# Building row one-hots for a dense gate matrix from a matrix product, with the gates multiplied into the column one-hots

## The chip, the core and the metric

The kernel runs on one core of a Trainium2 chip. The metric is the device time of one execution in microseconds (us); lower is better. The engines are PE (matrix products, with weight loads listed as PEld), DVE (the vector engine), ACT (the scalar engine, activations and copies), POOL (which here issues the gathers) and SP (which here issues the other DMAs).

## The reference, cut to what matters

One decoder layer over 512 tokens of width 1024: two attention groups, a layer norm, then a retrieval layer over 128 x 128 single-neuron experts, and a second layer norm. The change touches the retrieval layer:

```python
def peer_ffn(x, w_query, sub_keys, expert_u, expert_v):
    q = (x @ w_query).reshape(b, s_len, 8, 2, 128)
    scores = jnp.einsum('bshpc,hpnc->bshpn', q, sub_keys)
    top_s, top_i = lax.top_k(scores, 16)
    cand_s = top_s[..., 0, :, None] + top_s[..., 1, None, :]
    cand_i = top_i[..., 0, :, None] * 128 + top_i[..., 1, None, :]
    ...
    best_s, best_pos = lax.top_k(cand_s, 16)       # of 256 candidates
    expert_idx = jnp.take_along_axis(cand_i, best_pos, axis=-1)
    gates = jax.nn.softmax(best_s, axis=-1)
    ...
        h = jnp.einsum('td,ted->te', xb, expert_u[ib])
        act = gb * jax.nn.gelu(h, approximate=False)
        y = jnp.einsum('te,ted->td', act, expert_v[ib])
```

So each token has 8 x 16 = 128 selections ("slots"), each an expert (i1, i2) of the 128 x 128 grid and a gate.

## The kernel before

The 512 tokens are four blocks of 128. For blocks 0 and 1 the chosen rows of `peer_u` and `peer_v` are fetched one slot at a time by indirect DMAs (`gather`, issued by POOL; `gather_use` is the multiply-add on DVE, lines L805 and L818). For blocks 2 and 3 nothing is fetched by index: all 16384 experts stream through PE in 128 slabs. `h_mm` (and `run_ahead`, which does the same ahead of time, one of 8 parts at a call; L916) forms h for a slab and 256 tokens, `gelu` (L908) leaves its activation in `gl`, `act_prep` multiplies it by the gates, and `y_mm` (L1261) adds its product with `peer_v`.

For that, blocks 2 and 3 need the gates as a dense matrix: for each token a 128 x 128 matrix G[i2, i1] with a gate where a slot points and zero elsewhere. This is built in the **gate stage**, 64 steps of four tokens (`TG = 4`), in the loop `for s in range(NS)`. With the 128 slots of a token on the partitions, G of the token is one product of two f32 matrices, `o2` (slot x i2) and `o1` (slot x i1). A step consists of:

- `one_hot_b` (L867, DVE): compares the four tokens' row indices i1 with an iota, in bf16; tile `o1b`;
- `gated` (L882, ACT): four copies, one per token, of `o1b` into f32 `o1`, scaled by the gate of each slot;
- `one_hot_2` (L873, DVE): compares the column indices i2 with the iota, in f32; tile `o2`;
- `g_mm` (L888, PE): four products into one PSUM bank;
- `g_out` (L894, ACT): copies the bank into `stage`; every fourth step writes `stage` to the DRAM tile `gd` (SP) and keeps a part in `gt` (L898).

Between them the loop does one part of the routing of block 3 (`third`, a generator over `route_steps(3)`), and, when that has run out, parts of the last routing of block 1 (`late`) in the odd steps and one gather with its use (`gs`) in the others; and one or two parts of `run_ahead`. The order is the order of the code: each engine takes its instructions in program order, and buffers hold them back (`o2` has 2, `o1` and `o1b` have `GBUF = 3`).

`route_steps` ends, for blocks 2 and 3, with three transposes on PE (i1, i2 and the gates, so that slots come onto the partitions) and two copies on ACT: `s1` (bf16, i1) and `sg` (f32, i2 and gates). In it i1 is `i1`, and L753 to L760 derive i2 from the candidate's column (`eq`). Block 2's routing runs just ahead of the stage, with `run_ahead(KD)` and gathers in between.

Of the kernel before, what the change touches and what calls it, by code (L numbers as in the profile page):

```python
# [20 lines left out]
P = 128  # L21
# [3 lines left out]
NT = S // P  # L25
# [14 lines left out]
def make_consts():  # L40
    half = 8
    inv_freq = (np.float32(500000.0) ** (-np.arange(half, dtype=np.float32) * np.float32(2.0) / np.float32(16))).astype(np.float32)
    ang = np.arange(S, dtype=np.float32)[:, None] * inv_freq[None, :]
    c, s_ = np.cos(ang), np.sin(ang)
    cs = np.concatenate([c, c, -s_, s_], axis=1).astype(np.float32)
    cs = np.ascontiguousarray(cs.reshape(NT, P, 32).transpose(1, 0, 2))
    t = np.arange(P)[:, None]
    s = np.arange(P)[None, :]
    blocks = []
    for delta in range(NT - 1, -1, -1):  # L50
        d = delta * P + t - s
        mult = ((d >= 0) & (d <= 128)).astype(np.float64) + ((d >= 0) & (d % 4 == 0)) + ((d >= 0) & (d % 16 == 0))
        with np.errstate(divide="ignore"):
            blocks.append(np.where(mult > 0, -np.log(mult), -NEG))
    mask_a = np.concatenate(blocks, axis=1).astype(np.float32)
    mask_b = np.where(t < s, 0.0, NEG).astype(np.float32)
    tri = np.where(t >= s, -1.0, 0.0).astype(np.float32)
    offs = np.array(OFFS, np.float32)
    doff = np.diff(np.array([0] + OFFS, np.float32))
    iota = np.arange(16, dtype=np.float32)  # L60
    small = np.concatenate([offs, doff, iota, np.arange(P, dtype=np.float32)])
    small = np.ascontiguousarray(np.broadcast_to(small[None, :], (P, 48 + P)).astype(np.float32))
    return {"c_cs": cs, "c_maska": mask_a, "c_maskb": mask_b, "c_tri": tri, "c_small": small,
            "c_ident": np.eye(P, dtype=np.float32)}


# [6 lines left out]
TG = 4  # L73
# [8 lines left out]
GBUF = 3  # L82
# [12 lines left out]
def build(ctx, nc, tc, a):  # L95
# [11 lines left out]
    rp = open_pool(rqs, "rp", "right")  # L107
# [564 lines left out]
    def route_steps(tb, h0=0, n=PH):  # L672
        hs = slice(h0, h0 + n)
        ks = slice(h0 * 16, (h0 + n) * 16)
        NK = n * 16
# [34 lines left out]
        gt_ = (gate0, gate1)[tb][:, ks].rearrange("p (h k) -> p h k", h=n) if tb < 2 else rt([P, n, 16], "gate")  # L710
# [13 lines left out]
        i1 = rt([P, NK], "i1")  # L724
        i2 = rt([P, NK], "i2")
# [21 lines left out]
        nc.vector.tensor_mul(gt_, gt_, gz[:, :, None].to_broadcast([P, n, 16]))  # L747
        nc.vector.tensor_scalar(i1, i1, MAGIC, None, op0=OP.subtract)
        nc.vector.scalar_tensor_tensor(bob, i1, 64.0, bo, op0=OP.mult, op1=OP.subtract)
        for e in range(n // H2):  # L750
            sl = slice(e * HS, (e + 1) * HS)
            eq = rt([P, HS, 16], "eq", BF16)
            nc.vector.tensor_tensor(eq, bob[:, sl, None].to_broadcast([P, HS, 16]), smallb[:, None, 32:48].to_broadcast([P, HS, 16]), op=OP.is_equal)  # L753
            yield
            eqv = eq.rearrange("p (h k) j -> p h k j", h=H2)
            nc.vector.tensor_mul(eqv, eqv, topb[:, e * H2:(e + 1) * H2, None, :].to_broadcast(big))
            yield
            for w_ in (8, 4, 2):
                nc.vector.tensor_add(eq[:, :, :w_], eq[:, :, :w_], eq[:, :, w_:2 * w_])
            nc.vector.tensor_add(i2[:, sl], eq[:, :, 0], eq[:, :, 1])  # L760
            yield
# [3 lines left out]
                nc.vector.scalar_tensor_tensor(eidx[tb][e], i1[:, sl], float(P), i2[:, sl], op0=OP.mult, op1=OP.add)  # L765
            return
        tr = bank("tr").rearrange("p (j t) -> p j t", j=4)
        for j, s_ in enumerate((i1, i2, gt_.rearrange("p h k -> p (h k)"))):
            nc.tensor.transpose(tr[:, j], s_, ident)
        s1 = rp.tile([P, P], BF16, name="s1", bufs=2)  # L770
        sg = rp.tile([P, 2, P], F32, name="sg", bufs=2)
        nc.scalar.activation(s1, tr[:, 0], AF.Copy)
        nc.scalar.activation(sg, tr[:, 1:3], AF.Copy)
        gate[tb] = s1, sg
        yield

    def load_x2():
# [68 lines left out]
    tri = wcl("c_tri", [P, P])  # L846
# [10 lines left out]
    us, usp, gls, vs, vsp, acts, gts, gate = {}, {}, {}, {}, {}, {}, {}, {}  # L857

    steps = [(tb, t) for tb in (2, 3) for t in range(0, P, TG)]
    NS = len(steps)  # L860
    hot1, hot, hot2, gps, stages = {}, {}, {}, {}, {}

    def one_hot_b(s):
        if s < NS:
            tb, t = steps[s]
            hot1[s] = gb.tile([P, P, TG], BF16, name="o1b", bufs=GBUF)
            nc.vector.tensor_tensor(hot1[s], gate[tb][0][:, None, t:t + TG].to_broadcast([P, P, TG]), iob, op=OP.is_equal)  # L867

    def one_hot_2(s):
        if s < NS:  # L870
            tb, t = steps[s]
            hot2[s] = gb.tile([P, TG, P], F32, name="o2")
            nc.vector.tensor_tensor(hot2[s], gate[tb][1][:, 0, t:t + TG, None].to_broadcast([P, TG, P]),  # L873
                                    iota[:, None, :].to_broadcast([P, TG, P]), op=OP.is_equal)

    def gated(s):
        if s < NS:
            tb, t = steps[s]
            o1b = hot1.pop(s)
            hot[s] = gb.tile([P, TG, P], F32, name="o1", bufs=GBUF)  # L880
            for j in range(TG):
                nc.scalar.activation(hot[s][:, j], o1b[:, :, j], AF.Copy, scale=gate[tb][1][:, 1, t + j:t + j + 1])  # L882

    def g_mm(s):
        o1, o2 = hot.pop(s), hot2.pop(s)
        gps[s] = bank(("a", "b", "mm", "mm", "mm")[s % 5])
        for j in range(TG):
            nc.tensor.matmul(gps[s][:, j * P:(j + 1) * P], o2[:, j], o1[:, j], start=True, stop=True)  # L888

# [174 lines left out]
    with tc.manual_schedule():  # L1064
# [92 lines left out]
        stg = open_pool(sgs, "stg", "left", 2)  # L1157
        rq = open_pool(rqs, "rq", "right")
        gb = open_pool(rqs, "gb", "right", 2)
        iob = gb.tile([P, P, TG], BF16, name="iob", bufs=1)  # L1160
        nc.vector.tensor_copy(iob, iota[:, :, None].to_broadcast([P, P, TG]))
# [6 lines left out]
        run_ahead(KD)  # L1168
        run_ahead(KD)
        take(3)  # L1170
        one_hot_b(0)
        one_hot_b(1)
        gated(0)
        one_hot_2(0)
        third, late = route_steps(3), route_steps(1)
        for n in range(2):
            load_v(n)
        for s in range(NS):
            one_hot_b(s + 2)
# [226 lines left out]
```

## Time and profile before

| | |
|---|---|
| median of 3 runs | 1456.66 us (1455.78 to 1459.27) |
| the profiled execution | 1451.3 us, span 1449.5 us |
| granted PE clock, mean | 0.987 |
| PE busy | 1368.5 us (94%) |
| DVE busy | 1183.5 us (82%) |
| ACT busy | 494.2 us (34%) |
| POOL busy | 673.3 us (46%) |
| gate stage, first and last start of L867 | 590.0 to 715.0 us |

The profile is of one execution. Busy time counts records from start to end; records of one engine overlap a little where instructions follow without a wait. Idle time is put down to what ended it. The chain of waits goes back from the last instruction, at each step to what released it or to the instruction before it on its engine. Operands are written out<-in with partitions x elements; PE's f32 products appear as two records each.

### The profile page before, as it was taken

To read this page: it belongs to the slowest core of one execution; us is meant where nothing else is said; L and a number is where in the kernel's file an instruction comes from. 1 tells how busy PE (TensorE), PEld (TensorE's weight loads), DVE (VectorE), ACT (ScalarE), POOL (GpSimd) and SP (SyncE) were. 2 spreads that over 40 slices of the span, in tenths; PEclk is the share of its full clock that TensorE was granted. 3 is DMA by queue.
4 is the path that set the end of the run, shared out by engine and by line. 5 is a ranking of instruction groups with operands and counts; after the bars stand their busy time and mean duration, and the time that the engine had idled before them with its cause. 6 is when DMAs were issued, how large, how long until landed. Compare 5 with 4: busy or idle time off the path is not lost.

```text
span 1449.5 us, 19442 instructions
## 1 busy us (share of the span) xinstructions
PE 1368.5 (94%) x6602; PEld 1099.5 (76%) x6602; DVE 1183.5 (82%) x2444; ACT 494.2 (34%) x1010; POOL 673.3 (46%) x526
## 2 busy tenths in 40 slices
PE   8998999999989999988899999999989999998996
PEld 4676877677659998777688888888778888876565
DVE  1248988868888999999998778778778877888787
ACT  1312444454421111799722222222212222223232
POOL 0002477657643432114565555555556555656400
PEclk9999999999999999999999999999999999999998
DMA  8778899899879988769999999999999999999972
GB/s 300 224 266 303 276 366 316 286 350 380 302 294 339 326 285 313 268 195 301 297 405 409 410 410 409 410 410 409 410 409 411 408 410 410 409 410 409 374 282 85
DMA packets 162579, 495.92 MB, mean 342 GB/s; under 512 B 15376, under 2 KB 47520, under 8 KB 162480
## 3 DMA queue, kind: packets, MB, share of 16 engines
q0 software_dynamic: 74304, 270.13, 49.3%
q1 hardware_dynamic: 86448, 218.92, 41.1%
q10 hardware_dynamic: 1728, 5.64, 1.0%
q8 instruction: 52, 0.85, 0.2%
q14 instruction: 47, 0.39, 0.1%
HBM read 477.78 MB, written 16.84 MB: 341 GB/s over the span
## 4 chain that ended last, share of the span: by engine, by line
DMA 34%; DVE 27%; PE 26%; issue 7%; ACT 2%; POOL 2%; SPq 0%; DVEq 0%; POOLq 0%; ACTq 0%
DMA g<-peer_u,eidx 20%; DMA g<-peer_v,eidx 11%; PE y L1261 5%; DVE yg L818 4%; DVE x L818 3%; PE h L916 3%; PE m L269 2%; DVE o L873 2%; POOL g L796 2%; PE m L552 2%; PE tr L552 1%; DVE g L805 1%; DVE vl L126 1%; DVE o1b L867 1%; PE h L625 1%
## 5 line engine op out<-in xcount | busy, mean ns | idle before, releaser
L796 POOL DMA_INDIRECT g<-peer_v,eidx x256 | 336.1, 1313 | 353.7 <-DVE yg L818 102.7
L796 POOL DMA_INDIRECT g<-peer_u,eidx x256 | 331.3, 1294 | 346.3 <-DVE topi L601 125.1
L916 PE MATMUL h<-xf,w 128*128 128x256 f32 x2048 | 472.0, 380 | 4.4 <-ACT gl L908 4.4
L916 PEld LDWEIGHTS h<-xf,w 128*128 128x128 f32 x2048 | 383.2, 190 | 56.4 <-ACT gl L908 4.8
L805 DVE SCALAR_TENSOR_TENSOR g<-g,x 128x1024 f32<-128x1024 f32 x256 | 307.4, 1222 | 63.7 <-DMA g<-peer_u,eidx 63.0
L1261 PE MATMUL y<-vh,a 128*128 128x512 f32 x848 | 264.2, 415 | 15.0 <-ACT a L1244 14.0
L1261 PEld LDWEIGHTS y<-vh,a 128*128 128x128 f32 x848 | 158.1, 189 | 58.3 <-ACT a L1244 21.3
L818 DVE SCALAR_TENSOR_TENSOR yg<-g,hg,yg 128x1024 f32<-128x1024 f32 x126 | 161.5, 1282 | 24.3 <-DMA g<-peer_v,eidx 23.6
L818 DVE SCALAR_TENSOR_TENSOR x<-g,hg,x 128x1024 f32<-128x1024 f32 x128 | 163.8, 1280 | 21.2 <-DMA g<-peer_v,eidx 20.9
L126 DVE TENSOR_TENSOR vl<-v,vh 128x1024 fp32r<-128x1024 f32 x105 | 128.1, 1220 | 9.6 <-ACT vh L1209 9.5
L1244 ACT ACTIVATE a<-gl 128x512 fp32r<-128x512 f32 x53 | 33.4, 630 | 298.7 <-DVE gl L1234 298.7
L1261 PE MATMUL y<-vl,a 128*128 128x512 f32 x424 | 133.3, 396 | 0.0
L1209 ACT ACTIVATE vh<-v 128x1024 fp32r<-128x1024 f32 x105 | 110.5, 1052 | 24.9 <-DMA v<-peer_v 21.5
L908 ACT ACTIVATE gl<-h 128x256 f32<-128x256 f32 x128 | 48.3, 377 | 179.6 <-PE h L916 179.4
L1261 PEld LDWEIGHTS y<-vl,a 128*128 128x128 f32 x424 | 79.2, 188 | 19.3 <-DVE vl L126 1.6
L882 ACT ACTIVATE o<-o1b,sg 128x128 f32<-128x128 bf16 x256 | 83.7, 403 | 3.5 <-DVE o1b L867 3.5
L888 PEld LDWEIGHTS m<-o,o 128*128 128x128 f32 x304 | 38.7, 191 | 19.9 <-ACT o L882 15.3
L888 PE MATMUL m<-o,o 128*128 128x128 f32 x304 | 42.5, 283 | 11.4 <-ACT o L882 7.8
L269 PE MATMUL m<-w,x0f 128*128 128x256 f32 (+1 forms) x128 | 45.5, 505 | 5.0 <-DMA w<-w_in 5.0
L130 PE MATMUL m<-wl,x2h 128*128 128x512 f32 x96 | 39.9, 416 | 7.7 <-DVE wl L126 7.7
L873 DVE TENSOR_TENSOR o<-sg,c_small 128x512 f32<-128x512 f32 x64 | 43.8, 684 | 0.2 <-PE m L888 0.2
L1233 DVE TENSOR_TENSOR gl<-gl,gt 128x480 f32<-128x480 f32 x64 | 41.7, 651 | 0.0
(301 smaller groups left out, 1865.5 us busy)
## 6 DMA issues: line engine op xcount, KB each, us to landing
w<-uT SPq DMA_DIRECT2D x128, 512.0 KB, 9.1
v<-peer_v SPq DMA_DIRECT2D x108, 512.0 KB, 7.7
w<-w_in SPq DMA_DIRECT2D x47, 512.0 KB, 4.9
gt<-gd SPq DMA_DIRECT2D x15, 960.0 KB, 12.5
w<-peer_wq SPq DMA_DIRECT2D x16, 512.0 KB, 4.2
wq<-peer_wq SPq DMA_DIRECT2D x16, 512.0 KB, 6.8
gd<-stage SPq DMA_DIRECT2D x15, 512.0 KB, 5.3
gd<-stage SPq DMA_DIRECT2D x15, 448.0 KB, 4.2
```

The lines of the kernel that those rows point to most:

```text
L126: nc.vector.tensor_sub(parts[1], src, parts[0].bitcast(F32))
L269: nc.tensor.matmul(ps[:, ch * wd:(ch + 1) * wd], x0f[:, kk], w[:, k], start=kk == 0, stop=kk == KD - 1)
L796: nc.gpsimd.indirect_dma_start(out=u, out_offset=None, in_=a["peer_v" if kind else "peer_u"], in_offset=bass.IndirectOffsetOnAxis(ap=eidx[ ...
L805: nc.vector.scalar_tensor_tensor(u, u, 1.0, x, op0=OP.mult, op1=OP.mult, accum_out=hs[:, j:j + 1])
L818: nc.vector.scalar_tensor_tensor(acc, u, hs[:, j:j + 1], acc, op0=OP.mult, op1=OP.add)
L873: nc.vector.tensor_tensor(hot2[s], gate[tb][1][:, 0, t:t + TG, None].to_broadcast([P, TG, P]), iota[:, None, :].to_broadcast([P, TG, P]), ...
L882: nc.scalar.activation(hot[s][:, j], o1b[:, :, j], AF.Copy, scale=gate[tb][1][:, 1, t + j:t + j + 1])
L888: nc.tensor.matmul(gps[s][:, j * P:(j + 1) * P], o2[:, j], o1[:, j], start=True, stop=True)
L908: nc.scalar.activation(gls[c // 2][:, c % 2], ps[:, :ND], AF.Gelu)
L916: nc.tensor.matmul(hps[c][:, :ND], us[c][:, k], xf[:, k], start=k == 0, stop=k == KD - 1)
L1209: nc.scalar.activation(vsp[c][0], vs[c], AF.Copy)
L1261: nc.tensor.matmul(yps[t][hf], s_, w_[:, hf * 512:(hf + 1) * 512], start=c == 0 and n == 0, stop=c == P - 1 and n == len(terms) - 1)
```

## The change

The row one-hots are no longer compared on DVE. For an integer r and i = 0..127, 1 - (i - r)^2 is 1 at i = r and at most 0 elsewhere, so its Relu is the one-hot of r. Written out it is 2ir - r^2 + 1 - i^2, a sum of products of a term of r and a term of i. `route_steps` puts the terms of r into bf16 parts that are exact (r, r^2 rounded to bf16, and the rest), `parts`, and twelve small DMAs move them into `rows`: 32 tokens to a group, the three parts and a row of ones as the 128 rows of a matrix whose columns are the slots. The constant `c_w` (loaded as `cw`, 1 MB) holds the terms of i, laid out so that 512 columns pick four tokens out of a group.

- `same` (new, PE): one bf16 product of `rows` with 512 columns of `cw`, into bank m1 or m2;
- `one_hot_1` (new, ACT): Relu of the bank into `o1`, f32, in one instruction;
- `gated` (now on DVE): four `tensor_scalar`, one per token: iota equal to i2 of the slot, times the gate of the slot; tile `o2`;
- `one_hot_b`, `one_hot_2`, `o1b`, `s1` and `iob` go, and so does the transpose of i1;
- `g_mm` cycles over three PSUM banks in place of five.

DVE in the gate stage, from one step to the next, inside block 3's routing (L695 to L703 are its top-16 search, shifted by seven lines in the changed kernel). Before:

```order
L867 TENSOR_TENSOR o1b<-s_4525,iob 128x512
L873 TENSOR_TENSOR o_4692<-sg,c_small 128x512
L699 MATCH_REPLACE c_4673<-best,cand 128x50
L701 MAX best<-c_4671 128x8
L701 MAX best<-c_4673 128x8
L703 MAX_INDEX posu<-best,c_4671 128x8
L703 MAX_INDEX posu<-best,c_4673 128x8
L867 TENSOR_TENSOR o1b<-s_4525,iob 128x512
L873 TENSOR_TENSOR o_4717<-sg,c_small 128x512
L695 MAX best<-cand 128x8 x2
L697 MAX_INDEX posu<-best,cand 128x8 x2
```

Now, the same place (`sg` holds i2 and the gates, `c_small` the iota):

```order
L897 TENSOR_SCALAR o_4682<-c_small,sg 128x128 x4
L702 MAX best<-cand 128x8 x2
L704 MAX_INDEX posu<-best,cand 128x8 x2
L706 MATCH_REPLACE c_4687<-best,cand 128x50
L897 TENSOR_SCALAR o_4705<-c_small,sg 128x128 x4
L706 MATCH_REPLACE c_4689<-best,cand 128x50
L708 MAX best<-c_4687 128x8
L708 MAX best<-c_4689 128x8
L710 MAX_INDEX posu<-best,c_4687 128x8
L710 MAX_INDEX posu<-best,c_4689 128x8
L897 TENSOR_SCALAR o_4730<-c_small,sg 128x128 x4
```

The two comparisons of a step are replaced by four `TENSOR_SCALAR`, at the place where they stood.

PE from the end of block 2's routing into the stage. Before:

```order
L916 MATMUL h<-xf,w 128x256 x16
L888 MATMUL a<-o_4570,o_4575 128x128 x4
L916 MATMUL h<-xf,w 128x256 x2
L888 MATMUL b<-o_4581,o_4586 128x128 x4
L916 MATMUL h<-xf,w 128x256
L888 MATMUL m_4654<-o_4616,o_4621 128x128 x4
L916 MATMUL h<-xf,w 128x256 x2
L888 MATMUL m_4678<-o_4642,o_4647 128x128 x4
```

Now (`m` tiles without a number of their own in the code are banks m0, m1 and m2; L884 is `same`, L903 is g_mm, L931 a part of h):

```order
L931 MATMUL h<-xf,w 128x256 x16
L884 LDWEIGHTS rows
L884 MATMUL m_4582<-cw,rows 128x512
L884 LDWEIGHTS rows
L884 MATMUL m_4584<-cw,rows 128x512
L884 LDWEIGHTS rows
L884 MATMUL m_4595<-cw,rows 128x512
L903 MATMUL a<-o_4586,o_4588 128x128 x4
L931 MATMUL h<-xf,w 128x256 x2
L884 LDWEIGHTS rows
L884 MATMUL m_4630<-cw,rows 128x512
L903 MATMUL b<-o_4597,o_4599 128x128 x4
```

Three products of `rows` stand ahead of the first g_mm, and one ahead of each later one.

SP's queue from block 2's routing to the first write of `stage`. Before:

```order
L903 DMA w<-uT 128x1024 x17
L1061 DMA v_4198<-peer_v 128x1024
L1061 DMA v_4199<-peer_v 128x1024
L903 DMA w<-uT 128x1024
L897 DMA gd<-stage 128x7x128
```

Now:

```order
L918 DMA w<-uT 128x1024
L1176 DMA cw<-c_w 128x4096
L918 DMA w<-uT 128x1024 x14
L773 DMA rows<-parts 32x128 x12
L918 DMA w<-uT 128x1024 x2
L1076 DMA v_4198<-peer_v 128x1024
L1076 DMA v_4199<-peer_v 128x1024
L918 DMA w<-uT 128x1024
```

`cw` goes ahead of fourteen loads of u, and the twelve moves into `rows` stand ahead of the last two loads before the loads of v. Block 3's twelve stand in the same way among the stage's writes.

```diff
--- before.py
+++ after.py
@@ -60,7 +60,14 @@
     iota = np.arange(16, dtype=np.float32)
     small = np.concatenate([offs, doff, iota, np.arange(P, dtype=np.float32)])
     small = np.ascontiguousarray(np.broadcast_to(small[None, :], (P, 48 + P)).astype(np.float32))
-    return {"c_cs": cs, "c_maska": mask_a, "c_maskb": mask_b, "c_tri": tri, "c_small": small,
+    i, r = np.arange(P), np.arange(32)
+    w = np.zeros((P, 32, P), np.float32)
+    w[r, r] = 2 * i
+    w[32 + r, r] = w[64 + r, r] = -1
+    w[96] = -(i * i // P * P)
+    w[97] = 1 - i * i % P
+    w = w.reshape(P, 32 * P).astype(mybir.dt.np(BF16))
+    return {"c_w": w, "c_cs": cs, "c_maska": mask_a, "c_maskb": mask_b, "c_tri": tri, "c_small": small,
             "c_ident": np.eye(P, dtype=np.float32)}
 
 
@@ -747,11 +754,23 @@
         nc.vector.tensor_mul(gt_, gt_, gz[:, :, None].to_broadcast([P, n, 16]))
         nc.vector.tensor_scalar(i1, i1, MAGIC, None, op0=OP.subtract)
         nc.vector.scalar_tensor_tensor(bob, i1, 64.0, bo, op0=OP.mult, op1=OP.subtract)
+        if tb > 1:
+            parts = rt([P, 3, NK], "parts", BF16)
+            nc.scalar.activation(parts[:, 0], i1, AF.Copy)
+            nc.vector.tensor_mul(i1, i1, i1)
+            nc.scalar.activation(parts[:, 1], i1, AF.Copy)
+            rows = rp.tile([P, NT, P], BF16, name="rows", bufs=2)
+            nc.vector.memset(rows[96:], 1.0)
         for e in range(n // H2):
             sl = slice(e * HS, (e + 1) * HS)
             eq = rt([P, HS, 16], "eq", BF16)
             nc.vector.tensor_tensor(eq, bob[:, sl, None].to_broadcast([P, HS, 16]), smallb[:, None, 32:48].to_broadcast([P, HS, 16]), op=OP.is_equal)
             yield
+            if tb > 1 and e == 0:
+                nc.vector.tensor_sub(parts[:, 2], i1, parts[:, 1])
+                for g in range(NT):
+                    for j in range(3):
+                        nc.sync.dma_start(rows[32 * j:32 * j + 32, g], parts[32 * g:32 * g + 32, j])
             eqv = eq.rearrange("p (h k) j -> p h k j", h=H2)
             nc.vector.tensor_mul(eqv, eqv, topb[:, e * H2:(e + 1) * H2, None, :].to_broadcast(big))
             yield
@@ -765,13 +784,11 @@
                 nc.vector.scalar_tensor_tensor(eidx[tb][e], i1[:, sl], float(P), i2[:, sl], op0=OP.mult, op1=OP.add)
             return
         tr = bank("tr").rearrange("p (j t) -> p j t", j=4)
-        for j, s_ in enumerate((i1, i2, gt_.rearrange("p h k -> p (h k)"))):
+        for j, s_ in enumerate((i2, gt_.rearrange("p h k -> p (h k)"))):
             nc.tensor.transpose(tr[:, j], s_, ident)
-        s1 = rp.tile([P, P], BF16, name="s1", bufs=2)
         sg = rp.tile([P, 2, P], F32, name="sg", bufs=2)
-        nc.scalar.activation(s1, tr[:, 0], AF.Copy)
-        nc.scalar.activation(sg, tr[:, 1:3], AF.Copy)
-        gate[tb] = s1, sg
+        nc.scalar.activation(sg, tr[:, :2], AF.Copy)
+        gate[tb] = rows, sg
         yield
 
     def load_x2():
@@ -858,32 +875,30 @@
 
     steps = [(tb, t) for tb in (2, 3) for t in range(0, P, TG)]
     NS = len(steps)
-    hot1, hot, hot2, gps, stages = {}, {}, {}, {}, {}
-
-    def one_hot_b(s):
+    sps, hot, hot2, gps, stages = {}, {}, {}, {}, {}
+
+    def same(s):
         if s < NS:
             tb, t = steps[s]
-            hot1[s] = gb.tile([P, P, TG], BF16, name="o1b", bufs=GBUF)
-            nc.vector.tensor_tensor(hot1[s], gate[tb][0][:, None, t:t + TG].to_broadcast([P, P, TG]), iob, op=OP.is_equal)
-
-    def one_hot_2(s):
+            sps[s] = bank(("m1", "m2")[s % 2])
+            nc.tensor.matmul(sps[s], gate[tb][0][:, t // 32], cw[:, t % 32 * P:(t % 32 + TG) * P], start=True, stop=True)
+
+    def one_hot_1(s):
+        if s < NS:
+            hot[s] = gb.tile([P, TG, P], F32, name="o1", bufs=GBUF)
+            nc.scalar.activation(hot[s].rearrange("p j i -> p (j i)"), sps.pop(s), AF.Relu)
+
+    def gated(s):
         if s < NS:
             tb, t = steps[s]
             hot2[s] = gb.tile([P, TG, P], F32, name="o2")
-            nc.vector.tensor_tensor(hot2[s], gate[tb][1][:, 0, t:t + TG, None].to_broadcast([P, TG, P]),
-                                    iota[:, None, :].to_broadcast([P, TG, P]), op=OP.is_equal)
-
-    def gated(s):
-        if s < NS:
-            tb, t = steps[s]
-            o1b = hot1.pop(s)
-            hot[s] = gb.tile([P, TG, P], F32, name="o1", bufs=GBUF)
             for j in range(TG):
-                nc.scalar.activation(hot[s][:, j], o1b[:, :, j], AF.Copy, scale=gate[tb][1][:, 1, t + j:t + j + 1])
+                i2, g = (gate[tb][1][:, n, t + j:t + j + 1] for n in range(2))
+                nc.vector.tensor_scalar(hot2[s][:, j], iota, i2, g, op0=OP.is_equal, op1=OP.mult)
 
     def g_mm(s):
         o1, o2 = hot.pop(s), hot2.pop(s)
-        gps[s] = bank(("a", "b", "mm", "mm", "mm")[s % 5])
+        gps[s] = bank(("a", "b", "m0")[s % 3])
         for j in range(TG):
             nc.tensor.matmul(gps[s][:, j * P:(j + 1) * P], o2[:, j], o1[:, j], start=True, stop=True)
 
@@ -1157,8 +1172,8 @@
         stg = open_pool(sgs, "stg", "left", 2)
         rq = open_pool(rqs, "rq", "right")
         gb = open_pool(rqs, "gb", "right", 2)
-        iob = gb.tile([P, P, TG], BF16, name="iob", bufs=1)
-        nc.vector.tensor_copy(iob, iota[:, :, None].to_broadcast([P, P, TG]))
+        cw = gb.tile([P, 32 * P], BF16, name="cw", bufs=1)
+        nc.sync.dma_start(cw, a["c_w"])
         load_g(0)
         for i, _ in enumerate(route_steps(2)):
             if i < 14:
@@ -1168,17 +1183,17 @@
         run_ahead(KD)
         run_ahead(KD)
         take(3)
-        one_hot_b(0)
-        one_hot_b(1)
+        same(0)
+        same(1)
+        one_hot_1(0)
         gated(0)
-        one_hot_2(0)
         third, late = route_steps(3), route_steps(1)
         for n in range(2):
             load_v(n)
         for s in range(NS):
-            one_hot_b(s + 2)
+            same(s + 2)
+            one_hot_1(s + 1)
             gated(s + 1)
-            one_hot_2(s + 1)
             if next(third, third) is third:
                 if s % 2 == 0 or next(late, late) is late:
                     run(head(gs, 1))
```

## The prediction

> **What bounds the kernel now.** I read first the busy time by stage, then, for the stage that the change touches, the chain of waits, the groups, and the rows of single steps. The stages: the last of the routing of block 2 (530 to 590 us), the gate stage in two halves (590 to 636 and 636 to 720), the stream over the experts, and the tail. Columns are the stretch, its length, busy us of PE, weight loads, DVE, ACT and POOL with counts, granted clock, DMA share, GB/s.
>
> ```profile
> 530.00:590.00 60.00, 59.48 (x288) 52.38 (x287) 59.45 (x209) 10.92 (x24) 20.49 (x19) 1.00 0.86 291
> 590.00:636.00 46.00, 40.52 (x262) 35.00 (x261) 45.69 (x157) 45.16 (x132) 2.14 (x2) 1.00 0.69 227
> 636.00:720.00 84.00, 71.94 (x465) 59.75 (x464) 83.58 (x204) 78.51 (x226) 40.64 (x20) 1.00 0.91 284
> 720.00:1340.00 620.00, 604.08 (x2687) 506.91 (x2686) 505.69 (x652) 157.36 (x244) 357.53 (x268) 0.99 1.03 409
> ```
>
> In the gate stage DVE is busy 45.69 + 83.58 = 129.3 of 130 us and ACT 123.7; PE has holes, and DMA runs at 0.69 and 0.91. The stream behind it is held by DMA at 1.03 and 409 GB/s. The stage moves a fixed list of bytes and leaves the same buffers filled at its end, so microseconds cut from it should arrive at the end of the span, as long as it stays above its own DMA work: (46 x 0.69 + 84 x 0.91) / 1.03 = 105 us.
>
> The chain of waits in 590 to 720 by line, then the groups of that stretch:
>
> ```profile
> by line: DVE o L873 25.6%; DVE o1b L867 14.4%; ACT o L882 8.2%; DVE x L818 7.5%; issue 5.5%; DVE yg L818 4.7%; DVE eq L753 3.6%; ACT stage L894 3.4%; DVE eq L759 2.5%; DVE posu L697 2.3%; DVE posu L703 2.3%; DVE c L699 2.2%; DVE w L737 1.8%
> ```
> ```profile
> L873 DVE TENSOR_TENSOR o<-sg,c_small 128x512 f32<-128x512 f32 x64 | 43.8, 684 | 0.2 <-PE m L888 0.2
> L867 DVE TENSOR_TENSOR o1b<-s,iob 128x512 bf16<-128x512 bf16 x64 | 26.5, 416 | 0.0
> L882 ACT ACTIVATE o<-o1b,sg 128x128 f32<-128x128 bf16 x256 | 83.7, 403 | 3.5 <-DVE o1b L867 3.5
> ```
>
> The two one-hot comparisons lead, ACT's gate copies come next. DVE idles 0.2 us ahead of them: it sets the stage.
>
> **What one step costs now.** Records of neighbouring instructions overlap by some 0.08 us, so I take start to start. Two pieces of the chain (start, time on the chain, what), then a DVE step of the first half, from one L867 to the next:
>
> ```profile
> 590.08 0.67 DVE o1b L867 x2
> 590.75 0.60 DVE o L873
> ...
> 674.54 1.20 ACT o L882 x4
> 675.75 0.48 ACT stage L894
> ```
> ```profile
> 597.29 0.41 DVE L867 TENSOR_TENSOR o1b<-s,iob 128x512 bf16<-128x512 bf16 x1
> ...
> 599.00 0.42 DVE L867 TENSOR_TENSOR o1b<-s,iob 128x512 bf16<-128x512 bf16 x1
> ```
>
> L867 takes 0.335, L873 0.60, together 0.935 a step, 59.8 us in 64 steps; in that step 1.71 - 0.935 = 0.78 remain for routing. ACT needs 1.20 + 0.48 = 1.68 besides its gelu. PE over two steps:
>
> ```profile
> 595.62 1.05 PE L888 MATMUL m<-o,o 128*128 128x128 f32 x8
> 596.51 1.03 PE L916 MATMUL h<-xf,w 128*128 128x256 f32 x4
> 597.38 1.05 PE L888 MATMUL m<-o,o 128*128 128x128 f32 x8
> 598.27 0.60 PE L916 MATMUL h<-xf,w 128*128 128x256 f32 x2
> 598.70 0.50 PE L888 MATMUL m<-o,o 128*128 128x128 f32 x3
> ```
>
> 598.70 - 595.62 = 3.08 us without a wait: 1.54 a step (1.76 with two parts of h, 1.32 with one).
>
> **The change, part by part.**
>
> *DVE.* L867 and L873 go (59.8 us). In their place stand 256 TENSOR_SCALAR of 128x128 f32, each with two per-partition scalars. No such instruction is in the trace, so I bound it:
>
> ```profile
> 575.17 0.28 DVE L744 TENSOR_TENSOR bo<-bo,pos 128x128 f32<-128x128 f32 x1
> 575.37 0.20 DVE L745 RECIPROCAL gz<-gz 128x8 f32<-128x8 f32 x1
> 575.49 0.23 DVE L746 TENSOR_SCALAR i<-bo 128x128 f32<-128x128 f32 x1
> 575.63 0.28 DVE L747 TENSOR_TENSOR gate<-gate,gz 128x128 f32<-128x128 f32 x1
> ```
> ```profile
> L815 DVE TENSOR_SCALAR yg<-g,hg 128x1024 f32<-128x1024 f32 x2 | 1.5, 747 | 0.0
> L810 DVE TENSOR_SCALAR x<-x 128x1024 f32<-128x1024 f32 x2 | 1.4, 693 | 0.1
> L1161 DVE CAST iob<-c_small 128x512 bf16<-128x512 f32 x1 | 0.4, 407 | 0.0
> ```
>
> With two constants (L746) it takes 575.63 - 575.49 = 0.14: the lower end. One scalar read per partition adds 747 - 693 = 54 ns (L815 against L810), so one such read gives 0.19. If the second read is paid again, 0.245: the upper end with the same rate. I take 0.19, being nearest to the row with a per-partition scalar and supposing that the two reads overlap: 256 x 0.19 = 48.6 us, so DVE loses 11.2 us in the stage.
>
> By the Trainium skill (VectorE: DVE Perf Modes, section on the TRN2 errata) an SBUF to SBUF instruction takes 58 cycles plus elements over the mode's speed-up at 0.96 GHz; that is 0.127 us for the new form, and it would make the sum 256 x 0.127 = 32.5 us, a gain on DVE of 27. The trace agrees for L867 (0.327 by the rule, 0.335 here) and L873 (0.594, 0.60), but the rule has no term for a per-partition scalar, and L815 shows one. The same section says that the fixed part is paid by every instruction, so that many small tiles lose it many times; that speaks against four instructions in place of two.
>
> DVE also gets, in each routing of blocks 2 and 3, a multiply and a subtraction of 128x128 (0.20 each, L744) and a memset of 512 bf16 on 32 partitions (between 0.335 and 0.60, the two 512-wide rows; 0.5): 0.9 us each. Block 3's lies in the stage. Block 2's lies before it, where DVE and PE are both full; there L1161 goes (407 ns less the 0.08 of overlap: 0.32), leaving +0.6.
>
> *ACT.* Four copies (1.20) become one Relu out of PSUM over 128x512, priced as L894 (0.48): 0.72 less a step. ACT falls to 0.96 a step besides gelu and leaves the chain; worth nothing by itself, since DVE has no idle time that ACT ends. The two integer copies into `parts` (under 0.3 each) replace the copy into `s1`.
>
> *PE.* One bf16 product of 512 columns a step is added. The nearest row of that width in one pass is the y product of the stream:
>
> ```profile
> 903.67 1.08 PE L1261 MATMUL y<-vh,a 128*128 128x512 f32 x4
> 904.59 0.62 PE L1261 MATMUL y<-vl,a 128*128 128x512 f32 x2
> ```
>
> 904.59 - 903.67 = 0.92 for four: 0.23 each. Bounds: 0.11 (L888's 128 columns, (596.51 - 595.62) / 8) and twice 0.23. PE then needs 1.54 + 0.23 = 1.77 a step, 113 us in all, of a stage of 130. A transpose goes in each routing (some 0.1 us, left out). So PE stands close behind DVE, which comes to (130 - 11.2 + 0.9) / 64 = 1.87 a step. In the eight steps like the one above, DVE needs only 0.78 + 0.76 = 1.54 against 1.77, and `o2` has two buffers, so DVE cannot run far ahead: 8 x 0.23 = 1.8 us are lost. What is late next is g_mm, behind `same`.
>
> *Start.* Ahead of the stage PE finishes two slabs of h, then comes the first g_mm:
>
> ```profile
> 585.63 7.07 PE L916 MATMUL h<-xf,w 128*128 128x256 f32 x32
> ...
> 592.54 1.05 PE L888 MATMUL a<-o,o 128*128 128x128 f32 x8
> ```
>
> PE must now run `same` for three steps and ACT one Relu before that g_mm: 3 x 0.23 + 0.48, about 1.2 us later. DVE's third `gated` waits for the buffer that this g_mm reads, but DVE first has the candidate sums of block 3 to do; I take 0.4, with 0 and 1.2 as ends.
>
> *SP.* Twelve small DMAs per block go through its queue ahead of two loads of u.
>
> ```profile
> 574.40 15.21 SPq L903 DMA_DIRECT2D w<-uT  x5
> 589.70 0.86 SPq L1061 DMA_DIRECT2D v<-peer_v  x2
> ```
>
> At 0.43 each they hold SP for 5.2 us. It mostly waits there (5 loads in 15 us), and u is loaded three slabs ahead, of 7.07 / 2 = 3.5 us on PE before the stage and 10.8 in it (12 slabs in 130 us): covered; uncovered it would cost PE up to 5 us once. The rows themselves are wanted after the two slabs, 7 us behind the transposes, and their DMAs start ahead of the transposes; if they come late, the first g_mm is late by as much: 0 to 3 us, taken as 0. The 1 MB of `cw` is 2.6 us of DMA at 409 GB/s, in a stretch at 0.86: covered.
>
> *Sum:* -11.2 + 0.9 + 0.6 + 1.8 + 0.4 = -7.5 us. Against the profiled execution that is 1451.3 - 7.5 = 1443.8; it lies 5.4 under the median of the three runs, 1456.66, so for the median 1449.2.
>
> **Rivals.**
>
> *Two reads are paid twice* (slower). 0.245 each makes 62.7 us: +2.9 instead of -11.2. With 0.9, 0.6 and 0.4 (no loss to PE any more) +4.8: 1461.5. The sign turns where four instructions cost as much as the old pair less 1.9 / 64, at 0.226 each. For it: nothing shows the reads overlap. Against: a read is a latency of 54 ns, and two independent ones can share it.
>
> *PE becomes the bound.* If a per-partition scalar costs nothing at this size (0.14), DVE needs 130 - 59.8 + 35.8 + 0.9 = 106.9, and PE's 113, begun at 592.5, with the wait for one Relu sets the stage: 2.5 + 113 + 0.5 = 116; with 0.6 ahead of it that is -13.4: 1443.3. This is where the skill's rule above leads. L815 speaks against it.
>
> *The comparison loses the double rate.* L746 does 128 elements in 0.14; at half that rate, as L873 stands to L867, it is (0.60 - 0.335) / 4 = 0.07 more: 0.26 with one read and 0.32 with two, +9 to +24 us: 1466 to 1480. No row shows is_equal in this form.
>
> *The change doesn't reach the end.* The second half, 42 of the 64 steps, would go from 84 to 76.6 us, and DMA's share there from 0.91 to 1.00. If the gathers then come late to DVE, that half's 7.4 us are lost, and nothing remains of the sum: 1456.6. Against it: the stream runs at 1.03.
>
> **Numbers.** Chances: forecast 0.52 (own range 1445 to 1454), two reads 0.27, PE bound 0.10, single rate 0.05, DMA 0.06. A measurement can tell 0.3%, 4.4 us, from nothing. Faster: 0.48 of the forecast and 0.10: 0.58. Same: 0.04 of the forecast, half of two reads with 0.13, DMA's 0.06: 0.23. Slower: 0.14 and 0.05: 0.19. The range goes from the PE-bound case to just past two reads, 1443 to 1462.5; outside stay the single rate and the outer edges, some 0.12.
>
> **What would show it.** DVE: TENSOR_SCALAR 128x128 start to start at 0.19 (0.14 or 0.245 decide the rivals), 256 of them, stage near 122 us. ACT: Relu 0.48, idle in the stage. PE: the bf16 product 0.23, a few waits left. The stream unchanged at 1.03. Wrong would make it a price of the new form over 0.226, late rows that hold PE at the start, or a longer stream.

## The result and the profile after

The changed kernel is slower: 1473.4 us (median; 1468.03 to 1480.22) against 1456.7 us (1455.78 to 1459.27), a ratio of 1.0113 with a 95% interval of 1.008 to 1.0145. A second set of runs gave 1.0132 (1.0093 to 1.0172). The forecast was a ratio of 0.995, with 1449.2 us and a range up to 1462.5.

Busy time by stage in the changed kernel's profile (columns as in the prediction). The first line is the end of block 2's routing, the next two the time around a wait of PE, the fourth the gate stage from its first g_mm, the last the stream:

```profile
574.00:589.00 15.00, 15.00 (x71) 13.22 (x70) 9.74 (x15) 2.58 (x7) 3.35 (x2) 1.00 0.76 250
589.00:600.00 11.00, 3.61 (x17) 2.93 (x17) 10.30 (x18) 0.49 (x2) 2.49 (x2) 0.85 0.44 111
600.00:610.00 10.00, 9.32 (x37) 7.67 (x37) 7.63 (x23) 2.04 (x6) 4.55 (x4) 0.82 0.88 310
610.00:744.00 134.00, 123.07 (x768) 100.52 (x767) 131.60 (x469) 84.28 (x163) 17.82 (x19) 1.00 0.78 243
740.00:1340.00 600.00, 590.02 (x2631) 497.93 (x2632) 488.42 (x638) 150.75 (x238) 351.54 (x260) 0.99 1.02 407
```

Three things are to be seen. DVE still sets the stage (131.60 of 134 us), and the stage has grown. Ahead of it lies something that was not there: DVE is busy for only 9.74 of 15 us, then PE for only 3.61 of 11, and PE's granted clock drops to 0.85 and 0.82. The stream is as it was, with DMA at 1.02. The chain of waits in 604 to 744 us, by line, and then the groups of that stretch (busy us, mean ns of one, idle time ahead and what ended it):

```profile
by line: DVE o L897 45.2%; DVE yg L835 8.5%; DVE x L835 7.7%; PE h L931 4.9%; DVE w L744 2.9%; DVE eq L741 2.9%; DVE bo L747 2.9%; DVE c L706 2.2%; DVE posu L710 2.1%; DVE posu L704 2.1%; DVE eq L778 1.8%; DVE eq L767 1.7%; PE a L903 1.4%; 
```
```profile
L897 DVE TENSOR_SCALAR o<-c_small,sg 128x128 f32<-128x128 f32 x256 | 75.4, 362 | 3.8 <-PE a L903 3.3 <-PE b L903 0.4
L889 ACT ACTIVATE o<-m 128x512 f32<-128x512 f32 x64 | 38.0, 595 | 11.4 <-PE m L884 10.7
L884 PE MATMUL m<-cw,rows 128*128 128x512 bf16 x63 | 23.9, 379 | 5.9 <-ACT o L889 5.9
```

The 256 new instructions hold 45.2% of the chain; the two comparisons of before held 40.0%, of a shorter stretch. ACT's copies are gone from the list, as forecast. What four of the new instructions cost is read from start to start, as in the prediction. Two groups of the second half, the second one behind a use of a gathered row (L835):

```profile
729.48 1.11 DVE L897 TENSOR_SCALAR o<-c_small,sg 128x128 f32<-128x128 f32 x4
730.50 1.28 DVE L835 SCALAR_TENSOR_TENSOR yg<-g,hg,yg 128x1024 f32<-128x1024 f32 x1
731.69 1.34 DVE L897 TENSOR_SCALAR o<-c_small,sg 128x128 f32<-128x128 f32 x4
732.74 0.68 DVE L775 TENSOR_TENSOR eq<-eq,topb 128x1024 bf16<-128x1024 bf16 x1
```

The first group takes 730.50 - 729.48 = 1.02 us and the second 732.74 - 731.69 = 1.05. Added up in this way, with waits left out, the 256 instructions of the stage take 65.8 us, 0.257 each; the 128 comparisons of before take 60.0. So DVE loses 5.8 us in the stage, where the forecast gained 11.2.

The dip ahead of the stage, in the timeline (start, us, engine and line; in brackets the wait ahead and what ended it):

```profile
585.15 0.38 ACT L923 ACTIVATE gl<-h 128x256 f32<-128x256 f32 x1 [3.07 <-PE h L931]
588.60 0.38 ACT L923 ACTIVATE gl<-h 128x256 f32<-128x256 f32 x1 [3.07 <-PE h L931]
588.88 0.30 ACT L759 ACTIVATE parts<-i 128x128 bf16<-128x128 f32 x1
589.22 0.29 DVE L760 TENSOR_TENSOR i<-i 128x128 f32<-128x128 f32 x1 [5.37 <-ACT parts L759]
599.40 0.45 PE L788 MATMUL tr<-c_ident,i 128*128 128x128 f32 x1 [7.39 <-DVE i L779]
599.86 8.89 PE L931 MATMUL h<-xf,w 128*128 128x256 f32 x32
603.95 2.28 DVE L897 TENSOR_SCALAR o<-c_small,sg 128x128 f32<-128x128 f32 x8
609.87 1.05 PE L903 MATMUL a<-o,o 128*128 128x128 f32 x8
```

Follow it backwards. The square of i1 (L760) overwrites i1 in place, so it must wait until ACT has copied i1 into `parts` (L759). That copy takes 0.30 us, but it stands in ACT's queue behind two gelu copies (L923), and each of these waits for h from PE, which has run ahead in the code by several us of work. So DVE stands idle for 5.37 us, for a copy that nobody was meant to wait for; the transposes that end the routing come later by as much, and PE waits 7.39 us for them, where before it waited 0.5. After that its two slabs of h take 8.89 us instead of 7.07.

### The profile page after: what moved, and what is told of

It is laid out like the page before. It is cut to its first block, busy times and chain, and to the rows that moved or that the text cites. A ratio compares the mean times of both kernels' runs of the same rounds, so it can differ in the third digit from the quotient of the medians.

```text
span 1474.4 us, 19473 instructions
## 1 busy us (share of the span) xinstructions
PE 1391.7 (94%) x6663; PEld 1115.8 (76%) x6664; DVE 1191.4 (81%) x2577; ACT 457.1 (31%) x820; POOL 665.6 (45%) x526
## 4 chain that ended last, share of the span: by engine, by line
PE 41%; DMA 29%; DVE 18%; issue 6%; POOL 2%; ACT 2%; another core or an unknown queue 0%; SPq 0%; DVEq 0%; ACTq 0%; POOLq 0%
DMA g<-peer_u,eidx 17%; PE h L931 11%; DMA g<-peer_v,eidx 10%; PE y L1276 6%; DVE o L897 4%; PE a L664 3%; PE b L664 3%; PE m L276 2%; POOL g L813 2%; DVE yg L835 2%; PE m L559 2%; PE tr L559 1%; DVE x L835 1%; DVE g L822 1%; DVE vl L133 1%
## 5 line engine op out<-in xcount | busy, mean ns | idle before, releaser
L813 POOL DMA_INDIRECT g<-peer_v,eidx x256 | 318.2, 1243 | 397.7 <-DVE o L897 113.0
L813 POOL DMA_INDIRECT g<-peer_u,eidx x256 | 341.5, 1334 | 335.7 <-DVE topi L608 121.3
L931 PE MATMUL h<-xf,w 128*128 128x256 f32 x2048 | 475.4, 382 | 4.5 <-ACT gl L923 4.5
L931 PEld LDWEIGHTS h<-xf,w 128*128 128x128 f32 x2048 | 385.7, 192 | 57.6 <-ACT gl L923 5.0
L1276 PEld LDWEIGHTS y<-vh,a 128*128 128x128 f32 x848 | 159.4, 190 | 55.9 <-ACT a L1259 17.1
L835 DVE SCALAR_TENSOR_TENSOR x<-g,hg,x 128x1024 f32<-128x1024 f32 x128 | 167.4, 1308 | 20.7 <-DMA g<-peer_v,eidx 18.2
L835 DVE SCALAR_TENSOR_TENSOR yg<-g,hg,yg 128x1024 f32<-128x1024 f32 x126 | 165.2, 1311 | 22.9 <-DMA g<-peer_v,eidx 22.2
L133 DVE TENSOR_TENSOR vl<-v,vh 128x1024 fp32r<-128x1024 f32 x105 | 128.2, 1221 | 14.7 <-ACT vh L1224 14.5
L923 ACT ACTIVATE gl<-h 128x256 f32<-128x256 f32 x128 | 48.5, 379 | 227.6 <-PE h L931 219.6
L897 DVE TENSOR_SCALAR o<-c_small,sg 128x128 f32<-128x128 f32 x256 | 75.4, 362 | 3.8 <-PE a L903 3.3
L889 ACT ACTIVATE o<-m 128x512 f32<-128x512 f32 x64 | 38.0, 595 | 11.4 <-PE m L884 10.7
L276 PEld LDWEIGHTS m<-w,x0f 128*128 128x128 f32 x128 | 24.2, 197 | 21.4 <-issue 13.4
L138 PE MATMUL m<-wh,x2l 128*128 128x512 f32 x96 | 38.9, 407 | 0.0
```

The source lines that it names most:

```text
L133: nc.vector.tensor_sub(parts[1], src, parts[0].bitcast(F32))
L276: nc.tensor.matmul(ps[:, ch * wd:(ch + 1) * wd], x0f[:, kk], w[:, k], start=kk == 0, stop=kk == KD - 1)
L813: nc.gpsimd.indirect_dma_start(out=u, out_offset=None, in_=a["peer_v" if kind else "peer_u"], in_offset=bass.IndirectOffsetOnAxis(ap=eidx[ ...
L835: nc.vector.scalar_tensor_tensor(acc, u, hs[:, j:j + 1], acc, op0=OP.mult, op1=OP.add)
L897: nc.vector.tensor_scalar(hot2[s][:, j], iota, i2, g, op0=OP.is_equal, op1=OP.mult)
L923: nc.scalar.activation(gls[c // 2][:, c % 2], ps[:, :ND], AF.Gelu)
```

## How the loss was split

The executions start the routing of block 2 up to some us apart before the change has done anything (the traced run of the changed kernel was 7.4 us late there; a second one was early). So I set all traces to the cast that opens that routing (L682 before, L689 after):

```profile
552.64 0.29 DVE L682 CAST topf<-topi 128x256 f32<-128x256 uint32 x1
```
```profile
560.03 0.36 DVE L689 CAST topf<-topi 128x256 f32<-128x256 uint32 x1
```

From that cast to the first comparison of the stage is "routing"; from there to the start of the last step's g_mm is "stage". All times are in us, from one traced execution each; the ratio is that of the timed runs, against the kernel before in the same set of runs. There are three such sets, in which the kernel before took 1456.7, 1452.2 and 1450.4 us, so medians are compared within a set only.

| kernel | routing | stage | sum, against before | ratio (95% interval) |
|---|---|---|---|---|
| before | 37.4 | 128.0 | | |
| changed | 43.9 | 138.8 | +17.4 | 1.0113 (1.008 to 1.0145) |
| changed, second set | 44.4 | 138.1 | +17.1 | 1.0132 (1.0093 to 1.0172) |
| copies into `parts` on DVE | 38.9 | 137.3 | +10.8 | 1.0087 (1.0063 to 1.011) |
| one per-partition scalar, no gates | 44.3 | 123.9 | +2.9 | 1.0036 (1.0018 to 1.0053) |
| both of these | 38.9 | 123.0 | -3.5 | 1.0002 (0.9984 to 1.0021) |
| before, with ACT's copy alone | 43.0 | 130.0 | +7.7 | 1.0061 (1.0039 to 1.0084) |
| gates in the Relu, copies on DVE | 38.9 | 121.1 | -5.4 | 0.9962 (0.9939 to 0.9984) |
| the same, second set | 38.9 | 122.5 | -4.0 | 0.9981 (0.9961 to 1.0001) |

1% is 14.5 us. The two columns separate the two causes in the main: the wait moves the first by 5 to 6 us (and the second by 1 to 2), the price of the new instruction the second, and their sum reaches the end of the span.

## The experiments

**The two copies into `parts` on DVE**, the rest as changed:

```diff
-            nc.scalar.activation(parts[:, 0], i1, AF.Copy)
+            nc.vector.tensor_copy(parts[:, 0], i1)
             nc.vector.tensor_mul(i1, i1, i1)
-            nc.scalar.activation(parts[:, 1], i1, AF.Copy)
+            nc.vector.tensor_copy(parts[:, 1], i1)
```

> The changed kernel with its two integer copies into `parts` on DVE instead of ACT (0.14 us each), nothing else. Theory (the copies stand in ACT's queue behind gelu copies that wait for PE, so DVE waits 5.4 us for them, PE then 7.4 us for the transposes, and PE's clock is halved for 6.8 us after that idle time): the 5.4 us wait goes, the stage starts 6 to 7 us earlier, time 1473.4 - 7 = 1466 or somewhat less. Rival (the start is not what costs; the longer comparisons and a slower early part are all of it): 1472 to 1474.

Measured: 1465.15 us (1463.09 to 1467.08), 1.0087 of before. Its timeline:

```profile
577.14 0.29 DVE L760 TENSOR_TENSOR i<-i 128x128 f32<-128x128 f32 x1
587.60 0.30 PE L788 MATMUL tr<-c_ident,i 128*128 128x128 f32 x1 [1.93 <-DVE i L779]
592.15 2.29 DVE L897 TENSOR_SCALAR o<-c_small,sg 128x128 f32<-128x128 f32 x8
```

L760 waits for nothing, PE waits 1.93 instead of 7.39, and the routing is 5 us shorter. The stage stays long. So the wait is one cause: without it 6.6 of the 17.4 us in the traces are gone. The time of 1466 that was expected came out only because the kernel before, too, was faster in this set; by the ratios 3.8 us are gone (6.5 against the second set of the changed kernel), where 7 were expected.

**One per-partition scalar instead of two**, the rest as changed (the gates are left out of G):

```diff
-                nc.vector.tensor_scalar(hot2[s][:, j], iota, i2, g, op0=OP.is_equal, op1=OP.mult)
+                nc.vector.tensor_scalar(hot2[s][:, j], iota, i2, None, op0=OP.is_equal)
```

> The changed kernel with gates left out of the column one-hots: `tensor_scalar` compares with one per-partition scalar and doesn't multiply (the output lacks the gates). Theory that each per-partition read is paid: start to start goes from 0.255 to 0.20, 256 x 0.055 = 14 us less on DVE, the gate stage some 10 to 12 us shorter (PE then sets part of it), time 1462. Rival that 0.255 is a loss of the double rate, not a second read: 0.25 or more remains, time 1472.

Measured: 1457.48 us (1453.02 to 1462.0), 1.0036. The group of the new instructions, and the stage:

```profile
L897 DVE TENSOR_SCALAR o<-c_small,sg 128x128 f32<-128x128 f32 x256 | 55.3, 278 | 5.0 <-PE a L903 3.4 <-PE b L903 1.2 <-PE m L903 0.3
```
```profile
597.00:722.00 125.00, 118.62 (x788) 102.60 (x788) 119.28 (x489) 84.68 (x164) 21.00 (x21) 1.00 0.85 275
```

A record falls from 362 to 278 ns, from start to start an instruction takes 0.196 us in place of 0.257, and the stage is 15 us shorter, more than the 10 to 12 expected. Now DVE waits 5.0 us for g_mm, 3.2 of them at the start of the stage, and PE and DVE are both busy for 119 of 125 us: PE stands right behind. This edit takes the multiplication away together with the second scalar; the next run separates the two.

**The price by itself.** Five groups of 32 instructions at the end of the kernel before, where nothing else runs: no per-partition scalar, one, two; two at 64 columns; two with multiply and add instead of compare and multiply:

```diff
             run(final(t + 2))
+        for w_, ss, ops in ((P, 0, 0), (P, 1, 0), (P, 2, 0), (64, 2, 0), (P, 2, 1)):
+            for j in range(32):
+                one, two = ((3.0, 2.0) if ss == 0 else (gate0[:, j:j + 1], 2.0) if ss == 1
+                            else (gate0[:, j:j + 1], gate1[:, j:j + 1]))
+                nc.vector.tensor_scalar(hg1[:, :w_], iota[:, :w_], one, two,
+                    op0=(OP.is_equal, OP.mult)[ops], op1=(OP.mult, OP.add)[ops])
```

> The kernel before with 160 extra TENSOR_SCALAR behind the last layer norm: 32 each of 128 columns with two constants, with one per-partition scalar, with two, of 64 columns with two, and of 128 with two but multiply and add in place of compare and multiply. Theory of two paid reads at the double rate: 0.14, 0.19, 0.25, 0.21, 0.25 us start to start. Rival of a lost double rate for the comparison: 0.20, 0.25, 0.25 to 0.31, and 0.07 less with 64 columns.

Measured in one run, of which only these records are used; the four groups of that line (`hg` out, `c_small` the iota, `gate` the scalars; the 64 of the last row are compare with multiply and multiply with add together):

```profile
L1368 DVE TENSOR_SCALAR hg<-c_small 128x128 f32<-128x128 f32 x32 | 7.3, 227 | 1.1
L1368 DVE TENSOR_SCALAR hg<-c_small,gate 128x128 f32<-128x128 f32 x32 | 9.2, 286 | 1.1
L1368 DVE TENSOR_SCALAR hg<-c_small,gate,gate 128x64 f32<-128x64 f32 x32 | 10.0, 314 | 1.2
L1368 DVE TENSOR_SCALAR hg<-c_small,gate,gate 128x128 f32<-128x128 f32 x64 | 22.2, 346 | 2.3
```

227, 286, 346 ns: the first per-partition scalar costs 59 ns and the second 60. They do not overlap, and since all three groups do two operations, the multiplication is not what costs. 64 columns less save 32 ns, 0.5 ns a column, so the comparison runs at the double rate; that it loses it was another rival. Only the differences are used: each instruction here writes the same columns as the one before, which those of the stage do not, and from start to start they take 0.26, 0.32 and 0.38 us, longer than was expected.

**The changed kernel again**, in another set of runs, to see how much of its loss belonged to the one profiled run, which had lagged before the change began:

> The changed kernel once more, on the chip of the runs beside it. Theory: gate stage 139 to 140 us and 6 us more ahead of it, 16 to 17 us over the kernel before. Rival (part of the 16.7 us came from an early stretch of low clock that the change doesn't touch): with that stretch undisturbed only 9 to 11 us over.

Measured: 1470.11 us (1466.56 to 1470.81), 1.0132. DVE's wait and PE's after it are there again, without the early lag:

```profile
581.03 0.29 DVE L760 TENSOR_TENSOR i<-i 128x128 f32<-128x128 f32 x1 [5.88 <-ACT parts L759]
591.21 0.45 PE L788 MATMUL tr<-c_ident,i 128*128 128x128 f32 x1 [7.38 <-DVE i L779]
```

The stage was 138.1 us long and the routing 7.0 us longer than before. So the early lag is no part of the loss.

**Both undone**, the first two edits together (no gates in G here either):

> Copies into `parts` on DVE and one per-partition scalar in the comparison (gates left out of the output). If the two causes add up: the start of e1_parts_on_dve (stage begins 1 us late instead of 6) and the comparisons of e2_one_scalar (0.20 us), so 5 us under e2_one_scalar: ratio to the kernel before 0.9995 to 1.001. If they overlap, because a later start lets PE catch up, no better than e2_one_scalar: 1.0036.

Measured: 1450.77 us (1447.39 to 1453.8), 1.0002 with an interval of 0.9984 to 1.0021. The whole loss is gone, to within some 3 us, so no third cause of size is left. It is also the kernel that I had in mind when I predicted, with one scalar's price and no wait, and it is no faster than before; more on that below.

**ACT's wait alone, put into the kernel before.** Behind the line that forms `bob`, i1 goes through ACT and back; nothing else changes:

```diff
+        if tb > 1:
+            parts = rt([P, 2, NK], "parts", BF16)
+            nc.scalar.activation(parts[:, 0], i1, AF.Copy)
+            nc.vector.tensor_copy(i1, parts[:, 0])
```

> The kernel before with one thing of the change alone: in the routing of blocks 2 and 3, i1 is copied by ACT into a bf16 tile and back into i1 by DVE (values unchanged), so that DVE waits for ACT there. Theory: DVE waits about 5 us ahead of the stage, behind the gelu copies in ACT's queue, PE runs dry at the transposes, and the time rises by 5 to 8 us; in block 3 ACT's queue may add 1 to 3. Rival (DVE is ahead of PE by enough there, and the loss came from the DMAs into `rows` or from the load of `cw`): at most 1 us.

Measured: 1459.55 us (1454.67 to 1464.06), 1.0061. Its timeline, and the waits of DVE in block 2's routing:

```profile
579.77 0.38 ACT L912 ACTIVATE gl<-h 128x256 f32<-128x256 f32 x1 [3.07 <-PE h L920]
580.05 0.30 ACT L752 ACTIVATE parts<-i 128x128 bf16<-128x128 f32 x1
580.38 0.23 DVE L753 CAST i<-parts 128x128 f32<-128x128 bf16 x1 [5.55 <-ACT parts L752]
589.46 0.48 PE L773 MATMUL tr<-c_ident,i 128*128 128x128 f32 x1 [6.16 <-DVE i L764]
```
```profile
DVE i L753 <- ACT parts L752: 5.6, 1, 5.6
```

Two small instructions cost 0.6% in a kernel that has nothing else of the change: 8.8 us by the ratio, a little over the 5 to 8 expected, and 7.7 in the traces. In block 3's routing, within the stage, the same wait is 0.2 us: there ACT isn't held by PE in that way.

**The gates as the scale of the Relu**, with the copies on DVE: since g is positive, Relu(g x) = g Relu(x). Column one-hots are again one comparison over 128x512, and ACT runs one Relu per token:

```diff
-            nc.scalar.activation(hot[s].rearrange("p j i -> p (j i)"), sps.pop(s), AF.Relu)
+            ps = sps.pop(s)
+            for j in range(TG):
+                nc.scalar.activation(hot[s][:, j], ps[:, j * P:(j + 1) * P], AF.Relu,
+                                     scale=gate[tb][1][:, 1, t + j:t + j + 1])
...
-            for j in range(TG):
-                i2, g = (gate[tb][1][:, n, t + j:t + j + 1] for n in range(2))
-                nc.vector.tensor_scalar(hot2[s][:, j], iota, i2, g, op0=OP.is_equal, op1=OP.mult)
+            nc.vector.tensor_tensor(hot2[s], gate[tb][1][:, 0, t:t + TG, None].to_broadcast([P, TG, P]),
+                                    iota[:, None, :].to_broadcast([P, TG, P]), op=OP.is_equal)
```

> As e1_parts_on_dve, with the column one-hots compared by one 128x512 TENSOR_TENSOR again (0.60 us a step) and the gates as the scale of the Relu, four instructions of 128 columns out of PSUM. If a step's DVE work sets the stage: 0.60 against 1.02 in the changed kernel and 0.935 before, so 27 us less than the changed kernel on DVE, and PE (1.77 a step) or ACT (4 x 0.26 + 0.48 + gelu, about 1.8) sets the stage at 115 to 118 us, 12 less than before: 1446 to 1450. Rival (the stage's end is set by the DMAs or by the start, whatever DVE does): no faster than 1456.

Measured: 1447.22 us (1443.92 to 1451.14), 0.9962 (0.9939 to 0.9984). The same kernel on another chip:

> e4_gate_in_relu once more beside these: ratio 0.994 to 0.998 if its gain is the shorter stage (122 against 129 us); about 1 if that was its chip.

Measured: 1449.11 us (1445.05 to 1451.84), 0.9981 with an interval that reaches 1.0001. So the gain is 3 to 5.5 us, in the second set at the edge of what was expected, and the stage is 5.5 to 6.9 us shorter than before, where 12 were expected. The stage of the first of the two, and its groups on ACT and DVE:

```profile
588.00:710.00 122.00, 116.10 (x781) 101.62 (x781) 110.54 (x299) 111.87 (x353) 26.16 (x21) 1.00 0.86 283
```
```profile
L892 ACT ACTIVATE o<-m,sg 128x128 f32<-128x128 f32 x256 | 74.9, 410 | 4.2 <-PE m L884 4.1
L898 DVE TENSOR_TENSOR o<-sg,c_small 128x512 f32<-128x512 f32 x64 | 43.9, 687 | 10.6 <-PE a L905 4.9 <-PE b L905 2.8 <-PE m L905 2.3
```

DVE now waits 10.6 us for g_mm; PE, busy for 116 of 122 us, sets the stage, with ACT close behind (112). It is the best version here, a quarter of a per cent or so ahead of the kernel before, and the second set alone doesn't tell it from nothing.

## Why the prediction was wrong, point by point

**DVE's price: wrong, and the larger part of the miss.** The step was "supposing that the two reads overlap", with 0.19 us for an instruction and a gain of 11.2. The runs show 59 and 60 ns for the two reads, one after the other, and 0.257 us from start to start: a loss of 5.8, so 17.0 us of the miss. The argument that two independent reads can share a latency is refuted by the second 60 ns. That is the rival "two reads are paid twice", which had 0.245 and a chance of 0.27; its break-even of 0.226 was passed. The row with one scalar (L815 against L810, 54 ns) had the price of a read right; what I added to it, that a second one is free, no row showed. The Trainium skill's rule of 58 cycles plus elements over the speed-up (VectorE: DVE Perf Modes, TRN2 errata) gives an estimate of 0.127 us for this form; measured is twice that. That section's warning that many small tiles pay the fixed part each time is borne out: half the columns save only 32 of 346 ns.

**ACT's two copies: wrong, costed at nothing.** The step was that they "replace the copy into `s1`", with no term in the sum. That copy stood at the end of the routing, where only ACT's own result was waited for; the new ones stand in its middle, and DVE overwrites what they read. What I left out is the queue ahead of them on ACT, gelu copies bound to PE, and that DVE waits for its end. It cost DVE 5.4 to 5.9 us, and +0.61% (0.39 to 0.84) by itself; in the changed kernel 6.6 us of the traces.

**Routing of block 2: too small.** 0.6 was forecast; with no wait it is 38.9 - 37.4 = 1.5, of which some 0.4 are the two copies that this kernel has on DVE.

**Start: too small.** 0.4 was taken, with 1.2 as the upper end. DVE's third `gated` waited 3.3 us in the first trace, where PE's slabs ran in part at the lower clock, and 1.3 where the wait for ACT is gone and the slabs took 7.07 us:

```profile
DVE o L897 <- PE a L903: 3.3, 1, 3.3
```
```profile
DVE o L897 <- PE a L903: 1.3, 1, 1.3
```

**PE: price right, its closeness underrated.** The bf16 product takes 0.22 to 0.23 in the chain. But with nearly the price that I had supposed (one scalar, both causes undone) the stage shrinks by 5.0 us, not by the 8.1 that the terms in the stage add up to. About half of the difference is the price itself (0.196, not 0.19, in 256 instructions) and about half waits: DVE waits 3.6 us for g_mm there, 1.8 of them at the start, where 0.4 + 1.8 = 2.2 were taken. Where two engines are within 0.1 us a step of each other, as the forecast had them, steps of different content leave each waiting in turn. So even with both wrong steps put right the gain would have been 3.5 us in the trace and not measurable in time: -7.5 was too much on the small terms as well.

**SP: sized wrongly, covered.** The twelve DMAs hold its queue for 9.83 us, 0.82 each, where 5.2 was taken:

```profile
589.21 9.83 SPq L773 DMA_DIRECT2D rows<-parts  x12
599.14 6.53 SPq L918 DMA_DIRECT2D w<-uT  x2
608.59 0.38 PE L884 MATMUL m<-cw,rows 128*128 128x512 bf16 x1
```

PE goes from the two slabs of h to the first product of `rows` without a wait, so the rows were not late, and the loads of u behind them held nobody.

**Right:** DVE sets the stage; ACT leaves the chain; microseconds won or lost in the stage arrive at the end (sums of +17.4, +10.8, +2.9 and -3.5 us in the table against ratios that stand for 16, 13, 5 and 0); the comparison keeps the double rate; the stream is unchanged. The sum with the measured terms, 5.8 for the price, 0.9 and 1.5 for the routings, 1.7 for DVE's waits (1.3 at the start, 0.4 later), is 9.9, against 10.8 in the trace of the kernel without ACT's wait and 12.6 (9.1 to 16.0) by its ratio; the wait and what follows from it add the other 6.6 of the traces.

## What to carry to other kernels

Price an instruction by its form, with each per-partition operand counted on its own, and take a saving for granted only where a row shows it. Before an engine gets even a 0.3 us helper in the middle of a chain, look at what stands ahead of it in that engine's queue and for whom that waits: here a copy behind two gelus cost DVE 5 us, and on the engine that needed the result it cost 0.2. When an engine is relieved, ask at once which one is next, and by how much per step.

## What the hardware showed that I had not expected

*PE's clock after a pause.* Windows of 2 us around PE's wait of 7.39 us in the changed kernel (granted clock: third number from the end):

```profile
594.00:596.00 2.00, 0.00 (x0) 0.00 (x0) 1.90 (x5) 0.00 (x0) 0.21 (x1) 1.00 0.54 124
596.00:598.00 2.00, 0.00 (x0) 0.00 (x0) 1.97 (x4) 0.00 (x0) 0.48 (x1) 0.68 0.48 166
598.00:600.00 2.00, 0.59 (x3) 0.63 (x4) 1.90 (x5) 0.00 (x0) 0.67 (x1) 0.50 0.37 51
600.00:602.00 2.00, 2.00 (x7) 1.55 (x6) 2.00 (x3) 0.66 (x2) 1.28 (x1) 0.50 0.95 358
602.00:604.00 2.00, 2.00 (x7) 1.68 (x6) 2.00 (x3) 0.00 (x0) 1.40 (x2) 0.62 0.65 180
604.00:606.00 2.00, 2.00 (x11) 1.74 (x10) 2.00 (x10) 0.38 (x1) 1.69 (x2) 1.00 0.91 326
```

The clock is halved for some 6.8 us, from about 596.7 on, and for 4.1 of them PE is back at work (since 599.40); that is the 8.89 us of the two slabs against 7.07. The Trainium skill (TensorE: Matmul & The Clock Gate, Part 1) says that PE falls to half its clock after an idle window of about 3.4 us and comes back after as long a busy one; this trace agrees: the clock fell 4.7 us after the pause began and came back 4.1 us after it ended. But it also fell after a pause of only 1.95 us, in the second run of the best version:

```profile
585.24 0.30 PE L788 MATMUL tr<-c_ident,i 128*128 128x128 f32 x1 [1.95 <-DVE i L779]
```
```profile
588.00:590.00 2.00, 2.00 (x7) 1.55 (x6) 2.00 (x3) 0.00 (x0) 1.39 (x3) 0.50 0.54 122
```

Here the slabs took 8.76 us. In the first run of that version and in two other kernels, with pauses of 1.92 to 1.94 us, they took 7.07; what decides isn't shown.

*Two scalars beside a gather.* Where POOL issues a gather in the midst of a group of four, the fourth record lasts 0.55 us in place of 0.35. On the chain, where a piece runs to the end of its record, the groups right behind a use of a gathered row (18 of 58) therefore take 1.206 us on average and the other 40 take 1.032. It is hardly time lost: the next instruction starts nearly as early as ever, 1.045 us after the start of such a group against 1.019, some 0.5 us in the whole stage. With one scalar there is no such difference on the chain (0.791 for 15 and 0.794 for 31). What lengthens the record was not tried and stays open. So a price is better read from starts than from the pieces of the chain.
